# A gated recurrence on TensorE: the scores within 32 tokens in one run of 32-column tiles per head

## The chip, the core and the metric

One core of a Trainium2 chip. The metric is the device time of one execution in microseconds (us), the median of three runs. The engines are PE (TensorE, its weight loads as PEld), DVE (VectorE), ACT (ScalarE), POOL (GpSimd) and SP (SyncE).

## What is computed

Two transformer-like blocks on 512 tokens of width 1024, in float32. The change lies in the first block's recurrence, which the reference evaluates chunk by chunk for eight heads with 128 channels each:

```
f = sigmoid(zf); k = 1 - f; q = silu(zq); g = log f
S_t = diag(f_t) S_{t-1} + k_t v_t^T          (per head, S is 128 x 128)
o_t = S_t^T q_t
y   = rmsnorm(o) * norm_g * silu(zo)
```

Written out, a token t takes from each earlier token s the score `sum_c q[t,c] k[s,c] exp(G[t,c] - G[s,c])`, with G the running sum of g, times v_s.

## The kernel before

Activations lie transposed: 128 channels on the partitions, 512 tokens along a row. A main product (`mm_T`, L202 to L204, and `mm_N`, L242 to L244) multiplies a weight block by the activations in three passes, each operand being a high and a low half in fp32r. A weight block is loaded by SP, its high half cast by ACT (`wh`, L181) and its low half subtracted by DVE (`wl`, L182).

**The recurrence.** The decay from s to t is split by halving levels. At level n the tokens are cut into blocks of 2 x 2^n; the keys of a block's first half are decayed up to its middle, the queries of its second half from there. `Core.decays(n)` makes this tile, `dec`: POOL subtracts (two instructions, levels 0 to 5), or DVE adds up sums (levels 6 to 8), ACT takes the exponential, and DVE, or POOL for levels 1 and 3, multiplies by keys and queries. A product of keys with queries gives the level's scores. `Core.diag()` makes the scores of a token with itself, `Core.level(n)` those of level n: for n < 5 four products, one for each 128 tokens, each of 128 key columns with 64 query columns into PSUM, after which DVE copies under a mask into the score tile `sd` (L724). Level 5 goes through column tiles of 32 (`p[u:u + 32]`, u being 0 or 64), level 6 through 64 columns; levels 7 and 8 have tiles of their own (`l1`, `l2`). `Core.values()` multiplies the scores by the values, then `square`, `norm` and `done` norm and gate the head's output.

**The order.** `weave` writes two streams side by side: `main()` has the input products of heads 1 to 7 (`head_in`: forget gate zf, query zq, output gate zo) and the first three gates of the branches; `side()` has the recurrence of the heads. Each side step yields a cost that paces it against the main stream (`HGW`). `look(n)` writes decays ahead of their use. A scheduler then orders each engine's instructions, mainly as they are written; on the chip every engine works through its own list in that order.

Of the kernel before, what the change touches and what calls it, by code (L numbers as in the profile page):

```python
# [8 lines left out]
F32 = mybir.dt.float32  # L9
# [16 lines left out]
# buffers: raw weights, split weights, 2 KB tiles, small tiles, pairs of tiles, tiles of the attention  # L26
N_RAW = 4
N_W = 6
N_T = 54
# [11 lines left out]
CS = (0, 2, 6)  # L41
# [16 lines left out]
def tile_two_blocks(ctx: ExitStack, tc: tile.TileContext, a: dict, out: bass.AP):  # L58
# [197 lines left out]
    def weave(main, side, mt, st, late=False):  # L256
        """Emits two streams side by side, each at the pace of its length on the tensor engine."""
# [32 lines left out]
    # plan of all weights in the order of use  # L290
# [70 lines left out]
    # the small vectors, a chunk of 128 to a row; the first norm's come first  # L361
# [161 lines left out]
    # masks of the decay levels  # L523
    LV = [1, 2, 4, 8, 16]
    masks = cp.tile([128, len(LV), 64], U8, name="masks")

    def make_masks():
        for n, h in enumerate(LV):
# [8 lines left out]
            pool.tensor_copy(masks[:, n, :], m)  # L537

# [119 lines left out]
    class Core:  # L658
        """One head of the recurrence: the decays of the halving levels, scores, values."""
# [6 lines left out]
        def decays(self, n):  # L666
# [4 lines left out]
            e = T("dec")  # L671
# [20 lines left out]
        def diag(self):  # L692
            kq = self.kq
            p = PS("lv")
            for b in range(NT):
                bs = slice(b * 128, (b + 1) * 128)
                pe.matmul(p[:, bs], lhsT=kq[:, 0, bs], rhs=kq[:, 1, bs], start=True, stop=True)
            self.sd = T("sd")
            tt(dve, pieces(self.sd, 128), pieces(p, 128), ident.unsqueeze(1).to_broadcast([128, NT, 128]))

        def level(self, n):
            t = self.dec.pop(n)
            p = PS("lv")
            if n == 6:
                for b in range(NT):
                    pe.matmul(p[:64, b * 64:(b + 1) * 64], lhsT=t[:, b * 128:b * 128 + 64],
                              rhs=t[:, b * 128 + 64:(b + 1) * 128], start=True, stop=True)
                act.copy(pieces(self.sd, 128)[:64, :, 64:128], pieces(p[:64, :256], 64))
            elif n == 5:
                for b in range(2 * NT):  # L710
                    u = 64 * (b % 2)
                    pe.matmul(p[u:u + 32, b // 2 * 32:b // 2 * 32 + 32], lhsT=t[:, b * 64:b * 64 + 32],
                              rhs=t[:, b * 64 + 32:b * 64 + 64], start=True, stop=True)
                for u in (0, 64):
                    act.copy(pieces(self.sd, 128)[u:u + 32, :, u + 32:u + 64], pieces(p[u:u + 32, :128], 32))
            elif n < 5:
                hh = 1 << n
                nb = 64 // hh
                tv, sv = (z.rearrange("p (b q j i) -> p b q j i", b=NT, j=2, i=hh)[:, :, :, 1, :] for z in (t, self.sd))
                for b in range(NT):  # L720
                    pe.matmul(p[:, b * 64:(b + 1) * 64], lhsT=t[:, b * 128:(b + 1) * 128], rhs=tv[:, b],
                              start=True, stop=True)
                mk = masks[:, n, :].rearrange("p (q i) -> p q i", i=hh).unsqueeze(1).to_broadcast([128, NT, nb, hh])
                dve.copy_predicated(sv, mk, p[:, :256].rearrange("p (b q i) -> p b q i", b=NT, i=hh))  # L724
            elif n == 7:
                for b in range(2):
                    pe.matmul(p[:, b * 128:(b + 1) * 128], lhsT=t[:, b * 256:b * 256 + 128],
                              rhs=t[:, b * 256 + 128:b * 256 + 256], start=True, stop=True)
                self.l1 = T("l1", (128, 256))
                act.copy(self.l1, p[:, :256])  # L730
            else:
                for b in range(2):
                    pe.matmul(p[:, b * 256:(b + 1) * 256], lhsT=t[:, b * 128:(b + 1) * 128], rhs=t[:, 256:512],
                              start=True, stop=True)
                self.l2 = T("l2")
                act.copy(self.l2, p)
# [47 lines left out]
    def side():  # L784
# [13 lines left out]
        for h in range(8):  # L798
# [5 lines left out]
            look(9 * h + AHEAD)  # L804
# [3 lines left out]
            c.diag()  # L808
            yield 870
            for n in range(9):  # L810
                if ahead[0] <= 9 * h + n:
                    look(9 * h + n + 1)
                c.level(n)
                look(9 * h + n + 1 + AHEAD)
                yield 435 if 5 <= n < 8 else 870
                if h and n == CS[0]:
                    cores[h - 1].square()
                if h and n == CS[1]:
                    cores[h - 1].norm()
                if h and n == CS[2]:  # L820
                    cores.pop(h - 1).done()
# [36 lines left out]
    open_x(8)  # L858
    run(zi_half(0))
# [191 lines left out]
    # block-diagonal ones, causal mask, selector of a head's row  # L1051
# [15 lines left out]
    # f: log of the forget gates, summed over the tokens  # L1067
# [303 lines left out]
```

## Time and profile before

| | |
|---|---|
| median of three runs | 2157.38 us (2157.03 to 2157.44) |
| span of the profiled execution, first to last instruction | 2155.2 us |
| that execution's own time beside it | not recorded apart from the span |
| PE busy / DVE busy | 2119.9 us (98%) / 1243.4 us (58%) |
| ACT busy / POOL busy | 879.5 us (41%) / 522.9 us (24%) |
| first score product of head 0 / last of head 7 | 124.5 us / 359.0 us |

Busy shares are of the span. The shares of the whole span mix the recurrence, which has much work for DVE and POOL, with long stretches of plain products that have little.

### The profile page before, as it was taken

Reading aid. Unit: us, or ns where it says so; the run is one execution under the profiler, and the core shown is the slowest. Engines: PE = TensorE matmul, PEld = TensorE weight load, DVE = VectorE, ACT = ScalarE, POOL = GpSimd, SP = SyncE. Lnnn points to the kernel's source line nnn. Section 1 sums busy time; section 2 is a strip of 40 time slices with the busy share of each in tenths; the row PEclk is TensorE's granted clock in tenths of the full one; section 3 lists DMA queues with packets and bytes.
Section 4 is the critical chain, followed back from the end, with each engine's and each line's share of the span. In section 5 each row is a group of like instructions: output and inputs, shape, how many; then the busy total and the mean of one; then the engine's idle time right before and its main releaser. Section 6 shows DMA issues by size and latency. Waiting matters only on the chain.

```text
span 2155.2 us, 24922 instructions
## 1 busy us (share of the span) xinstructions
PE 2119.9 (98%) x9984; PEld 1739.5 (81%) x9984; DVE 1243.4 (58%) x1605; ACT 879.5 (41%) x1349; POOL 522.9 (24%) x446
## 2 busy tenths in 40 slices
PE   9999999999999999899999999999999999999999
PEld 7888777888888888688888888878877778888887
DVE  5588896555344443654555454568587755545453
ACT  6455555544323323332333232345466653323232
POOL 2537664012222222530111010020024411101000
PEclk9999999999999999999999999999999999999999
DMA  6311111232233332132322232232211112323321
GB/s 217 98 62 57 40 59 59 98 108 89 97 98 98 98 98 85 52 118 78 118 79 98 98 101 95 83 114 79 95 43 40 59 59 79 98 98 98 98 88 49
DMA packets 179180, 187.38 MB, mean 87 GB/s; under 512 B 4379, under 2 KB 169976, under 8 KB 179064
## 3 DMA queue, kind: packets, MB, share of 16 engines
q1 hardware_dynamic: 179048, 185.79, 26.6%
q8 instruction: 78, 1.28, 0.2%
q14 instruction: 38, 0.31, 0.0%
q10 hardware_dynamic: 16, 0.00, 0.0%
HBM read 183.68 MB, written 2.10 MB: 86 GB/s over the span
## 4 chain that ended last, share of the span: by engine, by line
PE 85%; DVE 7%; POOL 3%; ACT 3%; issue 2%; DMA 0%; SPq 0%; DVEq 0%; POOLq 0%; ACTq 0%
PE mm L202 25%; PE mm L203 25%; PE mm L204 25%; PE ao L1282 2%; POOL dec L107 2%; PE mn L244 1%; PE mn L243 1%; PE mn L242 1%; DVE wl L182 1%; ACT e L120 1%; DVE dec L107 1%; DVE sc L107 1%; PE pt L1270 1%; DVE e L110 1%; PE sc L1244 1%
## 5 line engine op out<-in xcount | busy, mean ns | idle before, releaser
L202 PE MATMUL mm<-xh,wh 128*128 128x512 f32 x2552 | 1006.6, 395 | 5.9 <-ACT xh L120 5.2
L203 PE MATMUL mm<-xl,wh 128*128 128x512 f32 x2552 | 999.2, 392 | 0.7 <-DVE xl L110 0.6
L204 PE MATMUL mm<-xh,wl 128*128 128x512 f32 x2552 | 998.5, 392 | 0.5 <-DVE wl L182 0.5
L181 ACT CAST wh<-raw 128x1024 fp32r<-128x1024 f32 (+2 forms) x355 | 363.5, 1025 | 783.5 <-PE mm L203 688.4
L182 DVE TENSOR_TENSOR wl<-raw,wh 128x1024 fp32r<-128x1024 f32 (+2 forms) x355 | 466.3, 1315 | 179.1 <-ACT wh L181 175.2
L202 PEld LDWEIGHTS mm<-xh,wh 128*128 128x128 f32 x2552 | 481.2, 189 | 106.9 <-ACT xh L120 6.1
L204 PEld LDWEIGHTS mm<-xh,wl 128*128 128x128 f32 x2552 | 480.6, 188 | 102.6 <-DVE wl L182 1.0
L203 PEld LDWEIGHTS mm<-xl,wh 128*128 128x128 f32 x2552 | 480.9, 188 | 100.5 <-DVE xl L110 2.0
L107 POOL TENSOR_TENSOR ua<-ua,rb 128x512 f32<-128x512 f32 x44 | 57.3, 1302 | 592.6 <-ACT ua L120 592.6
L107 DVE TENSOR_TENSOR x<-mm,x 128x512 f32<-128x512 f32 x64 | 44.1, 690 | 153.3 <-PE mm L204 153.3
L107 POOL TENSOR_TENSOR dec<-sc 128x256 f32<-128x256 f32 x96 | 89.5, 958 | 41.5 <-ACT kq L120 20.9
L107 DVE TENSOR_TENSOR a<-mm,rb 128x512 f32<-128x512 f32 x44 | 30.4, 691 | 103.5 <-PE mm L204 103.5
L107 POOL TENSOR_TENSOR acc<-acc,sq 128x512 f32<-128x512 f32 x42 | 62.8, 1495 | 103.9 <-ACT sq L120 82.0
L107 POOL TENSOR_TENSOR rl<-rl 128x512 f32<-128x512 f32 x32 | 49.0, 1532 | 129.3 <-ACT rl L120 129.3
L107 DVE TENSOR_TENSOR sg<-mm,ua 128x512 f32<-128x512 f32 x44 | 30.4, 690 | 84.3 <-POOL ua L107 81.8
L114 POOL TENSOR_SCALAR pe<-pe,rs 128x128 f32<-128x128 f32 (+1 forms) x32 | 31.1, 971 | 188.9 <-DVE rs L1262 184.1
L107 POOL TENSOR_TENSOR x<-x,rs 128x512 f32<-128x512 f32 x32 | 48.6, 1518 | 113.8 <-DVE rs L107 113.8
L110 DVE SCALAR_TENSOR_TENSOR xl<-x,vecs,xh 128x512 fp32r<-128x512 f32 x48 | 63.5, 1327 | 15.3 <-ACT xh L120 15.2
L110 DVE SCALAR_TENSOR_TENSOR ua<-a,convs,ua 128x511 f32<-128x511 f32 x88 | 65.8, 747 | 4.8 <-ACT ua L120 3.3
L242 PE MATMUL mn<-wh,xh 128*128 128x512 f32 x160 | 63.5, 404 | 0.0
L120 ACT ACTIVATE ua<-ua 128x512 f32<-128x512 f32 x44 | 27.8, 632 | 86.5 <-DVE ua L110 86.4
L243 PE MATMUL mn<-wl,xh 128*128 128x512 f32 x160 | 62.5, 391 | 0.0
(249 smaller groups left out, 2070.6 us busy)
## 6 DMA issues: line engine op xcount, KB each, us to landing
raw<-in_ffn_w_up_dram SPq DMA_DIRECT2D x44, 1024.0 KB
raw<-in_w_ff_dram SPq DMA_DIRECT2D x32, 1024.0 KB
raw<-in_w_in_dram SPq DMA_DIRECT2D x26, 1024.0 KB
raw<-in_ffn_w_down_dram SPq DMA_DIRECT2D x18, 1024.0 KB
raw<-in_a_w_in_dram SPq DMA_DIRECT2D x12, 1024.0 KB
raw<-in_w_kvf_dram SPq DMA_DIRECT2D x8, 1024.0 KB
raw<-in_b_w_qg_dram SPq DMA_DIRECT2D x8, 1024.0 KB
raw<-in_w_up_b_dram SPq DMA_DIRECT2D x4, 1024.0 KB
```

The lines of the kernel that those rows point to most:

```text
L107: e.tensor_tensor(out=o, in0=i0, in1=i1, op=op)
L110: dve.scalar_tensor_tensor(out=o, in0=i0, scalar=s, in1=i1, op0=op0, op1=op1)
L114: e.tensor_scalar(out=o, in0=i, scalar1=s1, scalar2=None, op0=op0)
L120: act.activation(out=o, in_=i, func=func, scale=scale, bias=bias, **kw)
L181: act.copy(hi, src)
L182: ins = dve.tensor_tensor(out=lo, in0=src, in1=hi.bitcast(F32), op=ALU.subtract)
L202: pe.matmul(ps, lhsT=lh, rhs=rh, start=start, stop=False)
L203: pe.matmul(ps, lhsT=lh, rhs=rl, start=False, stop=False)
L204: pe.matmul(ps, lhsT=ll, rhs=rh, start=False, stop=stop_)
L242: pe.matmul(pss[j], lhsT=xh[:, t0], rhs=wh[:, kk, :], start=(k + kk == 0), stop=False)
L243: pe.matmul(pss[j], lhsT=xh[:, t0], rhs=wl[:, kk, :], start=False, stop=False)
L1282: pe.matmul(o[64 * hA:64 * hA + 64, tb * 128:(tb + 1) * 128], lhsT=v[j][h // 8][:, (h % 8) * 64:(h % 8) * 64 + 64], rhs=et[:, j * 128:(j + ...
```

## The change

Diagonal and levels 0 to 4 (all scores within 32 tokens) become one run, `small()`: for each 32 tokens one product of 32 key columns, put into one of four column tiles of the array (32 partitions of PSUM each), with 32 query columns for the diagonal and 16 for a level. All scores of the run lie in one PSUM tile, 128 + 5 x 64 columns wide. DVE gathers them into a tile `s32` of 128 x 128 (one product with a folded identity, five copies under masks), and four copies, two on DVE and two on ACT, put them into `sd`. Levels 5 and 6 become a second run, `mid()`, level 6 now in two column tiles of 32; levels 7 and 8 a third, `far()`, unchanged but for the order. All five decays of the first run are written ahead of it. The decays get eight buffers of their own and the score tiles two, which are zeroed once; the pool of shared tiles goes from 54 to 51. The yielded costs and the pace follow the new steps.

```
-N_T = 54
+N_T = 51
-HGW = (130, 76)
+N_DEC = 8
+HGW = (130, 60)
...
-            e = T("dec")
+            e = xp[-1].tile([128, 512], F32, tag="dec", bufs=N_DEC, name=nm("dec"))
...
-        def diag(self): ...
-        def level(self, n): ...
+        def small(self):
+            kq = self.kq
+            p = PS("lv")
+            for b in range(NT):
+                for g in range(4):
+                    q = slice(b * 128 + 32 * g, b * 128 + 32 * g + 32)
+                    pe.matmul(p[32 * g:32 * g + 32, b * 32:b * 32 + 32], lhsT=kq[:, 0, q], rhs=kq[:, 1, q],
+                              start=True, stop=True)
+            for n in range(5):
+                t = self.dec.pop(n)
+                for b in range(NT):
+                    for g in range(4):
+                        q = slice(b * 128 + 32 * g, b * 128 + 32 * g + 32)
+                        c0 = 128 + 64 * n + 16 * b
+                        pe.matmul(p[32 * g:32 * g + 32, c0:c0 + 16], lhsT=t[:, q],
+                                  rhs=halves(t[:, q], 1 << n)[:, :, 1, :], start=True, stop=True)
+            s32 = T("s32", (128, 128))
+            tt(dve, pieces(s32, 32), pieces(p[:, :128], 32), id32.unsqueeze(1).to_broadcast([128, NT, 32]))
+            for n in range(5):
...
+                dve.copy_predicated(sv, mk, p[:, c0:c0 + 64].rearrange("p (b q i) -> p b q i", b=NT, i=hh))
+            self.sd = sds[self.h % len(sds)]
+            for g in range(4):
+                u = slice(32 * g, 32 * g + 32)
+                (act.copy if g % 2 else dve.tensor_copy)(pieces(self.sd, 128)[u, :, u], pieces(s32, 32)[u])
+        def mid(self):
+            p = PS("lv")
+            t5, t6 = self.dec.pop(5), self.dec.pop(6)
...
+            for b in range(NT):
+                for g in range(2):
+                    pe.matmul(p[32 * g:32 * g + 32, 128 + b * 64:192 + b * 64],
+                              lhsT=t6[:, b * 128 + 32 * g:b * 128 + 32 * g + 32],
+                              rhs=t6[:, b * 128 + 64:(b + 1) * 128], start=True, stop=True)
...
         for h in range(8):
-            look(9 * h + AHEAD)
+            look(9 * h + 5)
...
+            c.small()
+            yield 3200
...
+            look(9 * h + 7)
+            c.mid()
+            yield 700
...
+            look(9 * h + 9)
+            c.far()
+            yield 1300
...
+            look(9 * h + 9 + AHEAD)
             c.values()
```

On PE, head 0, between main products (`mm`), before: level 0 (`dec_953`) and level 1 (`dec_958`); `lv` is a score tile in PSUM.

```order
L721 MATMUL lv_1175<-dec_953 128x64 x4
L202 MATMUL mm_1146<-xh_353,wh_1059 128x512
L203 MATMUL mm_1146<-xl_354,wh_1059 128x512
L204 MATMUL mm_1146<-xh_353,wl_1060 128x512
L202 MATMUL mm_1204<-xh_145,wh_1102 128x512
L203 MATMUL mm_1204<-xl_146,wh_1102 128x512
L204 MATMUL mm_1204<-xh_145,wl_1103 128x512
L721 MATMUL lv_1208<-dec_958 128x64 x4
```

The same place in the changed kernel: diagonal (L704) and levels 0 to 4 (L712) in one piece.

```order
L204 MATMUL mm_1167<-xh_225,wl_1081 128x512
L704 MATMUL lv_1180<-kq_814 32x32 x16
L712 MATMUL lv_1180<-dec_969 32x16 x16
L712 MATMUL lv_1180<-dec_974 32x16 x16
L712 MATMUL lv_1180<-dec_979 32x16 x16
L712 MATMUL lv_1180<-dec_984 32x16 x16
L712 MATMUL lv_1180<-dec_989 32x16 x16
L202 MATMUL mm_1167<-xh_257,wh_1080 128x512
```

What were six runs with main products between them is one run of 96 products. Level 4, whose decay used to be needed last, now stands in the same run as the diagonal.

On POOL, the decays of head 5, before; the instructions that read `sc` are the two differences of a level, those that read `kq` the products of levels 1 and 3.

```order
L107 TENSOR_TENSOR dec_2365<-sc_2092 128x256 x2
L107 TENSOR_TENSOR dec_2370<-sc_2092 128x128x2 x2
L107 TENSOR_TENSOR dec_2375<-sc_2092 128x64x4 x2
L107 TENSOR_TENSOR dec_2388<-sc_2092 128x32x8 x2
L107 TENSOR_TENSOR dec_2370<-dec_2370,kq_2091 128x512
L107 TENSOR_TENSOR dec_2464<-sc_2092 128x16x16 x2
L107 TENSOR_TENSOR dec_2388<-dec_2388,kq_2091 128x512
```

The same in the changed kernel; the sixth row is level 5's, `osl` belongs to the norm of the head before.

```order
L107 TENSOR_TENSOR dec_2786<-sc_2418 128x256 x2
L107 TENSOR_TENSOR dec_2791<-sc_2418 128x128x2 x2
L107 TENSOR_TENSOR dec_2796<-sc_2418 128x64x4 x2
L107 TENSOR_TENSOR dec_2801<-sc_2418 128x32x8 x2
L107 TENSOR_TENSOR dec_2806<-sc_2418 128x16x16 x2
L107 TENSOR_TENSOR dec_2987<-sc_2418 128x8x32 x2
L107 TENSOR_TENSOR dec_2791<-dec_2791,kq_2417 128x512
L107 TENSOR_TENSOR osl_2650<-osq_2647,osh_2649 128x512
L107 TENSOR_TENSOR dec_2801<-dec_2801,kq_2417 128x512
```

The product of level 1 moved behind the differences of levels 4 and 5, that of level 3 behind these and `osl`.

## Rows read from the trace of the kernel before

**Rows 1.** The page, busy us, share of the span and instructions of each engine.
```profile
PE 2119.9 (98%) x9984; PEld 1739.5 (81%) x9984; DVE 1243.4 (58%) x1605; ACT 879.5 (41%) x1349; POOL 522.9 (24%) x446
```

**Rows 2.** Windows: length, busy us of PE, PEld, DVE, ACT, POOL; clock, DMA share, GB/s.
```profile
124.00:235.00 111.00, 110.64 (x682) 93.90 (x682) 94.97 (x122) 60.34 (x104) 61.62 (x58) 1.00 0.24 77
235.00:330.00 95.00, 85.49 (x513) 71.23 (x512) 89.04 (x108) 52.60 (x94) 60.21 (x54) 0.98 0.13 43
330.00:365.00 35.00, 32.65 (x189) 26.79 (x188) 28.04 (x38) 18.59 (x36) 17.99 (x17) 0.95 0.15 47
```

**Rows 3.** Waits, 235 to 330 us: who waited for whom, us in all, times, longest.
```profile
PE lv L733 <- DVE dec L107: 4.4, 2, 2.5
```

**Rows 4.** Timeline of PE: start us, us, line, operation; xN is so many instructions.
```profile
193.35 0.39 PE L243 MATMUL mn<-wl,xh 128*128 128x512 f32 x1
193.58 1.00 PE L721 MATMUL lv<-dec 128*128 128x64 f32 x8
...
194.70 0.39 PE L242 MATMUL mn<-wh,xh 128*128 128x512 f32 x1
...
195.85 0.40 PE L244 MATMUL mn<-wh,xl 128*128 128x512 f32 x1
196.18 0.45 PE L712 MATMUL lv<-dec 128*32 128x32 f32 x16
...
196.90 0.40 PE L243 MATMUL mn<-wl,xh 128*128 128x512 f32 x1
197.13 0.39 PE L244 MATMUL mn<-wh,xl 128*128 128x512 f32 x1
197.45 0.68 PE L706 MATMUL lv<-dec 128*64 128x64 f32 x8
...
198.40 0.39 PE L243 MATMUL mn<-wl,xh 128*128 128x512 f32 x1
```

**Rows 5.** Groups of PE by form, 90 to 365 us: busy us, mean ns of one.
```profile
L721 PE MATMUL lv<-dec 128*128 128x64 f32 x320 | 40.4, 269 | 2.6 <-DVE dec L107 2.4
L706 PE MATMUL lv<-dec 128*64 128x64 f32 x64 | 5.4, 227 | 0.2 <-DVE dec L107 0.2
L712 PE MATMUL lv<-dec 128*32 128x32 f32 x128 | 3.6, 199 | 0.0
```

**Rows 6.** Groups of DVE by form, 235 to 330 us.
```profile
L724 DVE COPY_PREDICATED sd<-masks,lv 128x256 f32<-128x256 uint8 x15 | 8.2, 550 | 0.1
L107 DVE TENSOR_TENSOR sd<-lv,ident 128x512 f32<-128x512 f32 x3 | 2.0, 677 | 0.0
```

**Rows 7.** Groups of DVE by form, whole span.
```profile
L1248 DVE TENSOR_REDUCE nmx<-sc 128x1 f32<-128x512 f32 x16 | 10.9, 681 | 5.6 <-PE sc L1246 5.6
L1248 DVE TENSOR_REDUCE nmx<-sc 128x1 f32<-128x128 f32 x16 | 4.6, 287 | 13.2 <-PE sc L1246 13.2
```

**Rows 8.** Timeline of POOL, 262 to 279 us.
```profile
262.45 7.35 POOL L107 TENSOR_TENSOR dec<-sc 128x256 f32<-128x256 f32 x8
...
272.15 2.26 POOL L107 TENSOR_TENSOR dec<-sc 128x256 f32<-128x256 f32 x2
...
275.05 1.67 POOL L107 TENSOR_TENSOR dec<-dec,kq 128x512 f32<-128x512 f32 x1 [0.63 <-ACT dec L120]
```

**Rows 9.** Timeline of DVE, 267 to 280 us.
```profile
269.21 0.68 DVE L107 TENSOR_TENSOR zf<-mm,rb 128x512 f32<-128x512 f32 x1
...
276.09 1.71 DVE L648 TENSOR_TENSOR_SCAN sc<-reset,g 128x512 f32<-128x512 f32 x1
```

**Rows 10.** The page, DMA queue of PE's instructions: packets, MB, share.
```profile
q8 instruction: 78, 1.28, 0.2%
```

**Rows 11.** Timeline of PE, 285 to 287 us.
```profile
285.45 0.40 PE L204 MATMUL mm<-xh,wl 128*128 128x512 f32 x1
285.81 0.45 PE L712 MATMUL lv<-dec 128*32 128x32 f32 x16
```

More of the change, by code (lines that the diff above doesn't have):

```diff
@@ L38 @@
 AHEAD = 4
+N_DEC = 8
 HGSTART = 36
-HGW = (130, 76)
-CS = (0, 2, 6)
+HGW = (130, 60)
 MUL_POOL = (1, 3)
@@ L524, in tile_two_blocks @@
     LV = [1, 2, 4, 8, 16]
-    masks = cp.tile([128, len(LV), 64], U8, name="masks")
+    masks = cp.tile([128, len(LV), 16], U8, name="masks")
+    id32 = cp.tile([128, 32], F32, name="id32")
     def make_masks():
+        dve.tensor_reduce(out=id32, in_=ident.rearrange("p (g c) -> p c g", g=4), axis=AX.X, op=ALU.max)
         for n, h in enumerate(LV):
@@ L536, in make_masks @@
                                pattern=[[2 * h, nb], [0, h]], channel_multiplier=-1)
-            pool.tensor_copy(masks[:, n, :], m)
+            r = SM("mr", 16)
+            dve.tensor_reduce(out=r, in_=m.rearrange("p (g c) -> p c g", g=4), axis=AX.X, op=ALU.max)
+            pool.tensor_copy(masks[:, n, :], r)
     gbc, bbc, sbc, wsn = T("lng"), T("lnb"), T("bs"), T("wsn")
@@ L690, in decays @@
             self.dec[n] = e
-        def diag(self):
+        def small(self):
             kq = self.kq
@@ L695, in diag @@
             for b in range(NT):
[L696 to L702, printed above, removed]
-            p = PS("lv")
[L704 to L736, printed above, removed]
@@ new lines, in small @@
+            self.sd = sds[self.h % len(sds)]
[3 more added lines that the diff above has]
+        def mid(self):
+            p = PS("lv")
+            t5, t6 = self.dec.pop(5), self.dec.pop(6)
+            for b in range(2 * NT):
+                u = 64 * (b % 2)
+                pe.matmul(p[u:u + 32, b // 2 * 32:b // 2 * 32 + 32], lhsT=t5[:, b * 64:b * 64 + 32],
+                          rhs=t5[:, b * 64 + 32:b * 64 + 64], start=True, stop=True)
+            for b in range(NT):
[3 more added lines that the diff above has]
+                              rhs=t6[:, b * 128 + 64:(b + 1) * 128], start=True, stop=True)
+            for u in (0, 64):
+                act.copy(pieces(self.sd, 128)[u:u + 32, :, u + 32:u + 64], pieces(p[u:u + 32, :128], 32))
+            act.copy(pieces(self.sd, 128)[:64, :, 64:128], pieces(p[:64, 128:384], 64))
@@ new lines, in far @@
+        def far(self):
+            t = self.dec.pop(7)
+            p = PS("lv")
+            for b in range(2):
+                pe.matmul(p[:, b * 128:(b + 1) * 128], lhsT=t[:, b * 256:b * 256 + 128],
+                          rhs=t[:, b * 256 + 128:b * 256 + 256], start=True, stop=True)
+            self.l1 = T("l1", (128, 256))
+            act.copy(self.l1, p[:, :256])
+            t = self.dec.pop(8)
+            p = PS("lv")
+            for b in range(2):
+                pe.matmul(p[:, b * 256:(b + 1) * 256], lhsT=t[:, b * 128:(b + 1) * 128], rhs=t[:, 256:512],
+                          start=True, stop=True)
+            self.l2 = T("l2")
+            act.copy(self.l2, p)
@@ L807, in side @@
                     yield None
[L808 to L821, printed above, removed]
+            c.small()
+            yield 3200
+            if h:
+                cores[h - 1].square()
+            look(9 * h + 7)
+            c.mid()
+            yield 700
+            if h:
+                cores[h - 1].norm()
+            look(9 * h + 9)
+            c.far()
+            yield 1300
+            if h:
+                cores.pop(h - 1).done()
+            look(9 * h + 9 + AHEAD)
             c.values()
@@ L858, in tile_two_blocks @@
     open_x(8)
+    sds = [xp[-1].tile([128, 512], F32, tag="sd", bufs=2, name=nm("sd")) for _ in range(2)]
+    for t in sds:
+        pool.memset(t, 0.0)
     run(zi_half(0))
```

5 lines of the change are left out of this document (added).

## Prediction

> **What bounds the kernel now.** I read the page's busy line first, then the windows around the recurrence, then single runs of products in the order of time.
>
> The busy line has TensorE at 98% of the span [rows 1]. A busy PE isn't a PE at its peak, so that row alone would let one think that any instruction taken off TensorE shortens the kernel. The windows show where that holds. I cut the recurrence near the first scores of heads 0, 4 and 7 [rows 2]. In the first window (four heads, 111 us) PE is busy for 110.64 us and DVE for 94.97, that is 86%: TensorE sets the pace. In the second (three heads, 95 us) PE falls to 85.49 and DVE rises to 89.04, 94%: there TensorE waits for VectorE, which has the decays' products, the weights' low halves and the gates to do. One wait shows it: the last level's products stand for VectorE's decay for 4.4 us in that window [rows 3]. In the third (35 us, head 7) neither is full. After it the program is plain products, which the change doesn't touch.
>
> So a microsecond saved on TensorE counts whole in the first window and hardly in the second, where one saved on VectorE counts instead.
>
> **What a run of scores costs now.** In the order of time, the main products start 0.23 us apart (196.90 to 197.13), and a level of a head is a run put between them [rows 4]. Its cost is the time from the main product ahead of it to the second one behind it, less two steps of 0.23. For one of the levels 0 to 4: 193.35 to 194.70 is 1.35, less 0.46 is 0.89, say 0.90. For level 5: 195.85 to 196.90 is 1.05, so 0.59. For level 6: 197.13 to 198.40 is 1.27, so 0.81. The diagonal has as many loads of 128 columns as a level, and I take 0.90 for it too. Per head: 6 x 0.90 + 0.59 + 0.81 = 6.8 us.
>
> **The new run, TensorE.** A product in f32 stands as two instructions (320 for the 160 calls of the levels 0 to 4 [rows 5]). The new first run has 16 products for the diagonal and 16 for each of five levels: 96 products, 192 instructions, each with 32 columns to load. The trace has one row of that form, level 5. Its 16 instructions lie in 0.45 us with a mean of 0.199 for one [rows 4, 5], so they start over 0.25 us, 15 gaps of 16.7 ns. The same sum for level 6 (64 columns) gives 0.68 - 0.227 = 0.45 over 7 gaps, 65 ns, and for a small level (128 columns) 1.00 - 0.269 = 0.73 over 7, 104 ns. From 64 to 32 columns the gap falls to a quarter, although the columns only halve. Level 5 alternates between two column groups (u = 0 or 64), level 6 doesn't: I read the other half as two column tiles working abreast. The new run turns through four groups, so its gap is between 16.7 ns (two abreast, as seen) and half of that, 8.3 (four abreast, argued, not seen); upwards the nearest row is level 6's 65. I take 16.7, the only row of this form: 192 x 16.7 ns = 3.2 us. The edges of such a run (what level 5 costs beyond its gaps) are 0.59 - 0.25 = 0.34. Together 3.5 us.
>
> The second run holds level 5 (0.25) and level 6 as 16 instructions that load 32 columns and stream 64, on two groups: 65 / 2 = 33 ns each, 0.52; one pair of edges, 0.34. Together 1.1 us. Levels 7 and 8 and the values are unchanged. In heads 4 to 7 the order puts one or two pieces of other work inside the first run, up to two more pairs of edges, 0.7 us, mostly in the window that VectorE sets; I leave them out. TensorE's bill falls from 6.8 to 4.6 us a head: 2.2 us, 17.6 for eight heads. Four abreast it is 1.9 + 1.1, so 3.8 us a head.
>
> **VectorE and ScalarE.** Now a head takes one product with the identity (0.68) and five predicated copies of 256 elements at 0.55, so 3.4 us [rows 6]. Afterwards these are one operation on 128 elements, five on 64, and two copies of 32 x 128; ScalarE takes two more copies, which it has room for. For the size I use the maxima, the same shape in 128 and 512 elements: 0.287 and 0.681 us [rows 7], so 1.03 ns an element and 0.155 fixed. That prices the first at 0.29, a copy at 0.29 at most, and a predicated copy between 0.155 + 0.066 = 0.22 and 0.55 - 192 x 1.03 ns = 0.35. The sum lies between 2.0 and 2.6; I take 2.3, a saving of 1.1 us a head.
>
> **What is moved.** Levels 0 to 4 used to be a run each, spread between main products, and a run needed only its own decay. Now the one run needs all five decays. What stands behind it on TensorE is every main product, so a late decay stops everything. GpSimd is the engine to look at: it makes the differences (eight in 7.35 us, two more in 2.26) and multiplies levels 1 and 3 (1.67 for one) [rows 8]. In the order of the changed kernel level 5's two differences stand ahead of these two products, so from the end of the scan to the last decay of the run are 7.35 + 2.26 + 2.26 + 2 x 1.67 = 15.2 us. Ahead of that lie VectorE's steps from the forget gate's product to the end of the scan, among other work: 269.21 to 277.80, 8.6 us [rows 9]. Together that's some 23.8 us, against about 26 us from one head's run to the next (a quarter of the first window as the sum below leaves it, 103.7 us). The forget gate's product of the next head ends just behind the run of this one. So the decays come just in time, and I charge 1.5 us of new waits to the first window, where nothing else would hide them. Moving the decays and score tiles into buffers of their own, and 51 instead of 54 shared tiles, I cost at nothing: the order behind the recurrence is the same but for single rows. If the tiles ran short, GpSimd's decays would start later and add to those 1.5 us.
>
> **Sum.** First window: 4 heads x 2.2 = 8.8, less 1.5, so 7.3 us; VectorE would then be at 90.6 of 103.7, 87%, still no bound. Second: VectorE's 89.04 less 3 x 1.1 is 85.7, at its present 94% a window of 91.5 instead of 95: 3.5 us. Third: head 7's own 2.2. Together 13.0 us. The profiled span of 2155.2 becomes 2142.2. The median of the runs lies 2.2 above that span, which I leave as it is: 2157.4 - 13 = 2144.4, so 2144 us.
>
> **Rivals.**
> *Four abreast.* For it speaks level 5's row: with two groups in turn the gap is a quarter of that with 64 columns. Against it: no row has four. First window 4 x 3.8 = 15.2 less 2 of waits (VectorE would be at 93%), second 4, third 3.8: 21 us, so 2136.
>
> *The waits eat the gain.* If GpSimd's 15.2 us come later than I put them, every head's run waits. At 1.6 us a head, 12.8 for eight, the 13 us are gone: 2157, the same. For it speaks the slack of some two microseconds; against it, that in the second window TensorE idles anyhow.
>
> *The long run is fed too slowly: slower.* The run is 384 instructions with the loads; the longest burst of this form that the trace shows has 32, and a burst can lie ready in a queue. TensorE's instructions come in packets, 78 of them with 1.28 MB in the span [rows 10], 16 KB each; for the 19,968 products and loads of the busy line that's 64 bytes each, 256 in a packet. One run is one and a half packets. It decides at 6.8 - 1.1 - 0.34 = 5.4 us for the 192, 28 ns an instruction. At 40 ns the run is 8.0 us, a loss of 2.3 a head and 18 us: 2176; at level 6's 65 ns a loss of 7.1 a head: 2214. Against it speaks a run of level 5 that came on an empty engine: at 285.81, 0.36 us behind the last start where 0.23 would do, its 16 still lie in 0.45 us [rows 11]. That run wasn't fed from a stock, but it was short.
> The Trainium skill, page "TensorE: Matmul & The Clock Gate", section "Back-to-back issue gap", gives small products a floor of about 25 ns from start to start whatever their size, and about 62 ns where the sequencer decodes them in software. By the first the run would be an estimated 5.1 us and the kernel some 5 us faster at most, by the second 12.2 us and the kernel about 50 us slower. This case's trace doesn't agree with either for a burst of 16 (16.7 ns); for 192 in a row no run here shows it.
>
> **How the numbers follow.** Chances: the sum as forecast, 7 to 19 us faster, 0.50; four abreast 0.18; waits that eat the gain 0.20, half of it within the bound; slow feeding 0.12. About 0.2% (4.3 us) is what a measurement of this kernel can tell from no change. Faster: 0.50 + 0.18 + 0.10 = 0.78; same 0.10; slower 0.12. The forecast's own range is 2138 to 2150. To leave out no more than two in ten it must take in most of four abreast and of the waits: 2131 to 2156.
>
> **What would show it.** Right: the first run's instructions start some 17 ns apart, and the run stands between main products for about 3.5 us; the predicated copies take 0.25 to 0.35; the time from the first scores of head 0 to those of head 4 falls by about 7 us, from there to head 7 by 3 to 4. Wrong: gaps above 28 ns, or holes inside the run; TensorE idle ahead of it, released by GpSimd's decays; no shorter second window, which would say that something other than VectorE's work sets it.

## The result and the profile after

The changed kernel takes 2181.91 us (median of 4 runs, 2179.91 to 2182.8) against 2157.2 of the kernel before: a ratio of 1.0114, interval 1.01 to 1.0129. It is slower by some 25 us where 13 us less were forecast. The profiled execution has a span of 2181.1 us, 25.9 above that of before.

Windows of the changed kernel, cut at the first scores of heads 0, 4 and 7 as in [rows 2] (length, busy us of PE, PEld, DVE, ACT, POOL, clock, DMA share, GB/s):
```profile
125.00:242.60 117.60, 103.48 (x1282) 84.11 (x1281) 95.89 (x134) 65.60 (x117) 66.33 (x65) 0.91 0.23 73
242.60:359.80 117.20, 84.40 (x989) 67.47 (x988) 84.71 (x116) 58.53 (x107) 61.80 (x57) 0.88 0.12 37
```
Cut exactly at the first scores, the windows before were 110.7 and 95.0, so 6.9 and 22.2 us are lost here. From head 7's scores to the first product of the norm that closes the mixer (the closing norm) it is 211.8 instead of 215.4, a gain of 3.6; behind that, 1609.5 against 1609.7. TensorE is less busy than before in both windows: it has less to do and waits more. The waits of PE from 124 to 385 us (in all, times, longest) say for what:
```profile
PE oss L789 <- ACT osh L784: 32.7, 5, 10.2
PE o L778 <- ACT l L753: 8.0, 5, 2.9
PE lv L712 <- issue: 4.2, 2, 2.3
```
`oss` is the norm product of the head before, `osh` the rounded square of its output. Neither was priced in the forecast. One such wait in the order of time, first PE, then ACT:
```profile
260.37 0.39 PE L204 MATMUL mm<-xh,wl 128*128 128x512 f32 x1
269.32 0.80 PE L789 MATMUL oss<-osh,onesr 128*128 128x512 f32 x1 [8.56 <-ACT osh L784]
269.92 1.06 PE L750 MATMUL lv<-dec 128*128 128x128 f32 x4
270.77 1.91 PE L757 MATMUL lv<-dec 128*128 128x256 f32 x4
```
```profile
262.82 0.63 ACT L120 ACTIVATE kq<-e 128x512 f32<-128x512 f32 x1 [1.21 <-DVE e L110]
263.64 0.63 ACT L120 ACTIVATE e<-zc 128x512 f32<-128x512 f32 x1 [0.18 <-DVE zc L114]
...
266.62 0.63 ACT L120 ACTIVATE dec<-dec 128x512 f32<-128x512 f32 x1 [1.31 <-POOL dec L107]
267.15 0.61 ACT L120 ACTIVATE sg<-e 128x512 f32<-128x512 f32 x1
267.67 0.58 ACT L120 ACTIVATE osq<-o 128x512 f32<-128x512 f32 x1
...
268.67 0.60 ACT L784 CAST osh<-osq 128x512 fp32r<-128x512 f32 x1
```
Look at `osq`, the square of the head before. Its input `o` was ready at 246.7 us, when the last values product ended. But on ScalarE it stands behind steps of the next head: the gate chain (`kq`, `e`, `sg`), which waits for VectorE (1.21 and 0.18 us), and two exponentials of decays, one of which waits 1.31 us for GpSimd. So it starts at 267.67. The change writes the square behind the whole first run and its 3200 columns, where the kernel before wrote it 1740 columns into the head; by then the weave has placed products of the next head, and so their gates, ahead of it. The norm product follows 700 columns later, ahead of the far levels, and behind it on TensorE stands everything. A wait can cost more than its length. Of these two stretches behind it, the first begins with the norm product:
```profile
269.30:274.00 4.70, 4.67 (x16) 4.06 (x17) 3.50 (x4) 2.41 (x4) 4.70 (x6) 0.62 0.00 0
274.00:278.00 4.00, 4.00 (x19) 3.30 (x18) 4.00 (x3) 0.00 (x0) 3.72 (x3) 1.00 0.00 0
```
After nearly nine idle microseconds the granted clock has a mean of 0.62 for 4.7 us (part of it at the lower of the two levels, 1.2 GHz) and is back at 1.00 (2.4 GHz) behind that.

The run itself is cheap. Timeline of PE around an undisturbed first run, and VectorE's merges by form, to set beside [rows 4 to 6]:
```profile
213.59 0.39 PE L204 MATMUL mm<-xh,wl 128*128 128x512 f32 x1
213.91 0.46 PE L704 MATMUL lv<-kq 128*32 128x32 f32 x32
214.19 1.62 PE L712 MATMUL lv<-dec 128*32 128x16 f32 x160
215.74 0.50 PE L202 MATMUL mm<-xh,wh 128*128 128x512 f32 x1
216.07 0.40 PE L203 MATMUL mm<-xl,wh 128*128 128x512 f32 x1
```
```profile
L712 PE MATMUL lv<-dec 128*32 128x16 f32 x1280 | 15.5, 189 | 4.2 <-issue 4.2
...
L722 DVE COPY_PREDICATED s<-masks,lv 128x64 f32<-128x64 uint8 x40 | 10.2, 254 | 0.9
```
By the forecast's own measure the run costs 216.07 - 213.59 - 0.46 = 2.02 us. The 160 instructions of the levels (80 products) lie in 1.62 us, 0.189 for one: (1.62 - 0.189) / 159 = 9.0 ns from start to start.

Not every run goes through like that. Heads 0 and 2 have a hole inside, in which TensorE waits for nothing that the profile shows. This is head 0's:
```profile
125.05 0.46 PE L704 MATMUL lv<-kq 128*32 128x32 f32 x32
125.32 1.45 PE L712 MATMUL lv<-dec 128*32 128x16 f32 x140
129.09 0.37 PE L712 MATMUL lv<-dec 128*32 128x16 f32 x20 [2.32 <-issue]
```
With their holes of 2.3 and 1.8 us these two runs take 4.4 and 3.9 us from first to last, those of heads 1 and 3 take 1.9. A packet of the queue that brings PE's instructions starts at 126.37 and at 187.92 us, 0.4 and 0.5 us ahead of the two holes; in heads 1 and 3 none starts before the run's last 0.3 us. In heads 4 to 6 the run is broken up by the values of the head before, which wait for their copies `l` inside it (0.7, 2.3 and 1.4 us).

### The profile page after: what moved, and what is told of

Its sections match the earlier page's. It is cut to its first block, busy times and chain, and to the rows that moved or that the text cites. A ratio compares the mean times of both kernels' runs of the same rounds, so it can differ in the third digit from the quotient of the medians.

```text
span 2181.1 us, 27350 instructions
## 1 busy us (share of the span) xinstructions
PE 2106.0 (97%) x11200; PEld 1720.9 (79%) x11200; DVE 1234.4 (57%) x1627; ACT 880.8 (40%) x1362; POOL 515.5 (24%) x448
## 4 chain that ended last, share of the span: by engine, by line
PE 87%; DVE 6%; POOL 3%; ACT 2%; issue 1%; DMA 0%; SPq 0%; POOLq 0%; DVEq 0%; ACTq 0%
PE mm L202 25%; PE mm L203 25%; PE mm L204 25%; PE ao L1310 2%; PE mn L243 2%; PE mn L244 2%; PE mn L242 2%; POOL dec L107 2%; DVE dec L107 1%; PE pt L1298 1%; DVE wl L182 1%; DVE sc L107 1%; POOL x L107 1%; PE sc L1272 1%; PE ml L229 1%
## 5 line engine op out<-in xcount | busy, mean ns | idle before, releaser
L107 POOL TENSOR_TENSOR dec<-sc 128x256 f32<-128x256 f32 x96 | 82.5, 892 | 75.0 <-DVE sc L652 51.8
L107 DVE TENSOR_TENSOR dec<-dec,kq 128x512 f32<-128x512 f32 x56 | 55.5, 1012 | 17.0 <-ACT dec L120 16.2
```

Of the source, the lines that this page charges most:

```text
L107: e.tensor_tensor(out=o, in0=i0, in1=i1, op=op)
```

## The experiments

For each kernel: time; the stretches from head 0 to 4, from 4 to 7, from 7 to the closing norm, by the first scores in its profiled execution; their sum. The kernel before was run beside each group of experiments and took 2157.0 to 2158.5 us, so a difference of one or two microseconds between two rows says nothing. The stretches from 4 to 7 and from 7 on have the same main products in most rows but trade time with each other: together they are 310 us in before, e1_runs_apart and e3_apart_buf.

```
                          us      0-4    4-7   7-norm    sum
before                  2157.2   110.7   95.0   215.4   421.0
after                   2181.9   117.6  117.2   211.8   446.5
e1_sq_early             2161.4   112.3  100.8   212.7   425.7
e1_norm_late            2178.3   110.0  114.5   215.1   439.6
e1_old_tiles            2186.9   121.0  116.1   212.6   449.7
e3_before_cs            2187.8   119.8  114.0   217.0   450.8
e1_runs_apart           2157.9   111.0  100.7   208.9   420.6
e2_apart_twice          2174.1   119.3  101.6   217.5   438.4
e3_apart_buf            2157.5   111.0   95.5   214.6   421.1
e3_apart_ahead5         2152.1   106.3   97.9   210.3   414.6
e4_before_ahead5        2159.6   111.3   97.9   214.7   423.9
e4_no_merge             2158.0   104.9  100.2   211.4   416.5
e5_mul_dve              2144.8   103.3   93.6   211.5   408.4
e5_pairs                2152.8   104.9   97.0   214.4   416.3
```

**What makes the loss.** Theory A: the new places of square and norm. Rivals: the long run is dear in itself (B); five decays are wanted at once (C). Four kernels are to tell them apart. The square ahead of the first run, nothing else:
```
+            if h:
+                cores[h - 1].square()
             c.small()
             yield 3200
-            if h:
-                cores[h - 1].square()
```


> One edit to the changed kernel: the square of the head before (ScalarE, with the copy that follows it) is issued ahead of the first run of a head instead of behind its 3200 columns; its norm product stays ahead of the run of the two far levels. Theory A (order: TensorE stands at the norm product because ScalarE reaches the square only behind the next head's gate chain; 32.7 us of waits in five places of the changed kernel): these waits all but vanish, the first scores of heads 0 to 7 lie about 200 to 205 us apart instead of 235, and the time is 2145 to 2160. Theory B (the long run of 192 small products is itself too dear): nothing changes, 2178 to 2186. Theory C (five decays wanted at once: TensorE and GpSimd wait on each other at the first run): the norm waits go but the same time comes back ahead of the run, 2170 or more.

2161.39 us, ratio 1.0019 (1.0009 to 1.0028). 20 of the 25 us are back, a little less than A said (the scores of heads 0 and 7 lie 213 us apart, not 200 to 205); C, which had the time come back ahead of the run, falls. The waits of PE from 125 to 385 us:
```profile
PE mm L202 <- ACT xh L478: 7.9, 1, 7.9
PE lv L712 <- issue: 6.3, 3, 2.5
PE mn L242 <- DVE z L107: 5.1, 1, 5.1
PE o L778 <- ACT l L753: 4.7, 4, 1.9
PE oss L789 <- ACT osh L784: 3.3, 1, 3.3
```
The norm wait fell from 32.7 to 3.3; other waits took its place, the longest 7.9. The holes given as issue are now three, 6.3 us in all, more than the 3 to 4 us by which this kernel is still behind the kernel before; each begins 0.4 to 0.6 us behind the start of a packet of PE's instructions. What the kernel would take without them was not tried.

The norm product behind the far levels, the square still late:
```
-            if h:
-                cores[h - 1].norm()
             look(9 * h + 9)
             c.far()
             yield 1300
             if h:
-                cores.pop(h - 1).done()
+                cores[h - 1].norm()
             look(9 * h + 9 + AHEAD)
             c.values()
+            if h:
+                cores.pop(h - 1).done()
```


> One edit to the changed kernel: the norm product of the head before is issued behind the run of the two far levels instead of ahead of it, and what follows it behind the values; the square stays late on ScalarE. Theory A: TensorE has the far run and some 1300 columns of main products more before it stands, so part of the 32.7 us of waits goes, at most about 5 x 1.8 us; but the chain on ScalarE is as late as before: 2165 to 2180. If the place of the product alone were to blame and not the square's place on ScalarE: 2150 to 2160. Theory B and C: 2178 to 2186.

2178.26 us, ratio 1.0095. That time lies within A's range and just within that of B and C, so it doesn't choose between them; it rules out that the place of the product alone is to blame. The wait, of which A wanted a part gone, stays whole, with 2000 columns between square and norm product:
```profile
PE oss L789 <- ACT osh L784: 34.6, 5, 14.1
```

The order of the change with the 128-column products and merges of before (`mid` then calls levels 5 and 6, `far` 7 and 8):
```
         def small(self):
+            self.diag()
+            for n in range(5):
+                self.level(n)
```


> The order of the changed kernel (one run for the diagonal and levels 1 to 16, one for 32 and 64, square behind the first, norm ahead of the far levels) with the products of the kernel before, 128 columns wide, and its masks. Theory A: as slow as the changed kernel or slower, 2180 to 2210, with the wait at the norm product of 25 us or more in sum. Theory B: the loss goes with the small tiles, so 2150 to 2165.

2186.88 us, ratio 1.014, with the norm wait in it:
```profile
PE oss L780 <- ACT osh L775: 26.6, 5, 9.5
```
The loss is there without one small tile, and B falls. The small tiles save 5 us in this order.

And the other way round, the kernel before with nothing but this, which writes the square of the head before behind level 3 instead of 0, its norm product behind level 4 instead of 2:
```
-CS = (0, 2, 6)
+CS = (3, 4, 6)
```


> The kernel before with three numbers changed and nothing else: the square of the head before is issued behind level 3 of the next head instead of level 0 (45% of the head's columns instead of 18%), its norm product behind level 4 instead of level 2; the last step stays. No product, mask or decay changes. Theory A (the place of square and norm alone makes the loss): 2172 to 2190, with 20 us or more of waits of TensorE at the norm product. If the loss needs the single long run too: 2155 to 2165.

2187.83 us, ratio 1.0144 (1.0127 to 1.0161). Two numbers, no product touched, and 31 us are lost: A holds without the long run, although the new places are not quite those of the change. The waits are not as expected: PE stood 11.9 us at the norm product, not 20, and 6.5 at the values, where it hadn't stood before; its waits for decays fell from 11.1 to 6.2. Its windows from head 0 to 4 and 4 to 7:
```profile
124.50:244.30 119.80, 114.17 (x687) 96.36 (x686) 88.13 (x119) 60.55 (x104) 55.52 (x54) 0.99 0.22 71
244.30:358.20 113.90, 98.47 (x536) 80.82 (x535) 88.90 (x114) 56.49 (x99) 65.24 (x59) 0.91 0.12 38
```
In the second, PE is 13 us busier than in [rows 2], at a clock of 0.91 instead of 0.98. It has 24 main products more there, 5.5 us at 0.23 each; the scores and values are the same, so some 7 us are left. Part of a wait's price appears as busy time.

**Where the tiles' gain is.** With the loss explained, the question is why the cheap run gave nothing. The small tiles in the old order, the diagonal and each level a run of its own, level 6 as before, square and norm in their old places:
```
+            c.diag()
+            yield 870
+            for n in range(9):
...
+                c.level(n)
```


> The small tiles of the changed kernel (four 32-column tiles abreast for the scores within 32 tokens) in the order of the kernel before: the diagonal and each level a run of its own, square and norm where they stood before, four decays ahead, level of 64 as before. Theory A (order, not tiles): no norm wait over 2 us, TensorE about 0.3 us cheaper for each of six runs of a head and VectorE's merges on 64 elements instead of 256: 2130 to 2150. Theory B (small products too dear in themselves): six short runs of 32 products each cost as much as the one of 192, so 2175 or more.

2157.89 us, ratio 0.9999 (0.999 to 1.0009), outside both expectations. A run of 16 small products (32 instructions) costs 0.58 where 128-column products cost 0.90, and not a microsecond is seen. The waits from 124 to 385 us:
```profile
PE o L768 <- ACT l L744: 9.4, 3, 5.9
PE o L768 <- ACT l L750: 4.7, 1, 4.7
PE o L768 <- DVE sd L726: 3.4, 1, 3.4
```
By this list, TensorE's saving is given back at the values, 17.5 us of waits for late copies; e3_apart_buf below shows that this can't be all. More room ahead of the values, the same order:
```
-                yield 435 if 5 <= n < 8 else 870
+                yield 435 if 5 <= n < 8 else 2000 if n == 8 else 870
...
             c.values()
-            yield 2180
+            yield 1050
```


> The small tiles in the order of before (e1_runs_apart, 2157.9 us, where TensorE waited 17.5 us at the values for ScalarE's copies l and VectorE's sd) with 2000 instead of 870 columns of main products ahead of the values and 1050 instead of 2180 behind them. Theory A2 (TensorE's saving of about 15 us is given back at these waits): the waits fall under 5 us and the time is 2140 to 2150. Rival (the stretch is bounded by VectorE and by the in-order chain between VectorE and ScalarE, TensorE's saving is off the path): the waits move elsewhere, 2154 to 2161.

2158.0 us, as the rival said, but not because the waits moved: those at the values fell only to 13.5, and the one at the input of a main product rose from 2.6 to 7.1. So the edit didn't take away what it was meant to. Two like edits in the changed order with the square early gave nothing either: more columns ahead of the values (2161.17, with the waits there up from 7.4 to 16.6), and the next head's decays one by one (2161.47):
```
-            yield 1300
+            yield 2400                 e2_early_slack; behind the values 1080
-            look(9 * h + 9 + AHEAD)
+            look(9 * h + 10)           e2_early_spread; + 11, 12 and 13 further on
```


> The changed kernel with the square early (as in e1_sq_early, 2161.4 us) and one more edit: between the run of the far levels and the values stand 2400 columns of main products instead of 1300, and 1080 instead of 2180 behind the values. Theory A2 (what is left after the square is moved is waits of TensorE for ScalarE's late copies l and sd ahead of the values product, 7.4 us, plus the 7.9 us at an input of the next main product which is late for the same reason): the value waits go, 2150 to 2157. Theory D (VectorE's bursts are what is left: TensorE's pieces wait where VectorE must read a finished product first): no change, 2158 to 2165.

> The changed kernel with the square early (2161.4 us) and one more edit: the four decays of the next head that were issued all together behind the far levels are issued one by one over the same columns of main products. Theory D (bursts: five decays behind each other on VectorE, 6 to 7 us in the chain of waits, hold up the reading of main products): 2148 to 2157. Theory A2: no change, 2158 to 2165.

Each small product issued twice (`for _ in range(2):` around both):

> The small tiles in the order of before (2157.9 us) with each of the 192 small products of a head issued twice; the output stays the same. It prices TensorE's columns: alone the second 192 take 8 x 6 x about 0.37 = 18 us. If TensorE bounds the stretch: 2170 to 2177. If its time there is off the path: 2157 to 2163. A run price as for instructions one after the other (rival: products fed too slowly, 28 ns or more each) would be 43 us, so 2185 or more.

2174.14 us: 16 us for the second 192 instructions of each head. By the table, 8.2 us of it lie between heads 0 and 4 and 9.5 behind head 4. So TensorE's time is on the path in this kernel, in both stretches: made dearer it costs at once. Made cheaper it gave nothing; that something else of nearly the same length takes over is the likely reading, not a shown one.

The decays back in the common pool, 55 buffers instead of 8 of their own:
```
-            e = xp[-1].tile([128, 512], F32, tag="dec", bufs=N_DEC, name=nm("dec"))
+            e = T("dec")
```


> The small tiles in the order of before (2157.9 us) with the decays in the common pool of small tiles again (55 buffers) instead of 8 buffers of their own. In the run with 8 of its own GpSimd stood 37 us at decays for TensorE's reading of an old one, with squares and gates queued behind. Theory E (those 8 buffers eat the gain): the GpSimd wait falls under 10 us and the time is 2142 to 2152. Otherwise (VectorE and ScalarE's in-order chain bounds): 2154 to 2161.

2157.46 us: buffers were not it. The waits did change, though. GpSimd's 37.0 us of waits for TensorE to read an old decay are gone, and of TensorE's 17.5 us at the values this is left:
```profile
PE o L768 <- ACT l L744: 0.4, 1, 0.4
```
Instead TensorE waits for VectorE's decays (13 us) and at the norm product (5.3), and the time is the same. So the waits at the values say where the saving went in one order, not why it was lost. GpSimd's half of the square one level later, and six decays ahead instead of four, gave nothing either (2161.52 and 2156.93, both outside what was expected):
```
+                if h and n == CS[0] + 1:
+                    cores[h - 1].rest()        e3_apart_osl: osl stands here
-AHEAD = 4
+AHEAD = 6                              e4_ahead6
```


> As e3_apart_buf, and GpSimd's half of the split square (osl) is issued one level later, so that GpSimd has a decay to do while ScalarE makes its input (before: 23 us of GpSimd waits there, 52 us with the small tiles). If GpSimd's queue holds up the decays: 3 to 8 us below e3_apart_buf. If not: within 3 us of it.

> Small tiles, order of before, six decays ahead. In the run with five TensorE still stood 13.7 us for decays of VectorE and GpSimd. If lead is what is lacking: 2145 to 2150. If VectorE has no more to give: 2150 to 2156.

The first of these two needs 418.7 us up to the closing norm, 2.4 less than e3_apart_buf, and loses 5.5 behind it, where the code is the same; e4_no_merge, below, loses as much there. Why, stays open.

Five decays ahead instead of four, with the small tiles and with the old ones:
```
-AHEAD = 4
+AHEAD = 5
```


> As e3_apart_buf with five decays ahead instead of four. If TensorE's runs now come too early for the elementwise engines, more lead gives the waits at the values back: 3 to 8 us below e3_apart_buf. If VectorE's share bounds the stretch, the same or up to 5 us above, since decays then stand ahead of the gate chain that main products wait for.

> Control: the kernel before with five decays ahead instead of four, old products and masks. If the 5 us that five ahead gave with the small tiles (2152.1) is lead alone: also 2150 to 2154 here. If it is the tiles' saving becoming usable: 2155 to 2162 here.

2152.14 us with the tiles (ratio 0.9972, 0.9961 to 0.9983), 2159.64 with the old ones (1.0012). So it isn't lead as such: at five ahead the tiles are worth 7.5 us, at four nothing. Five is one setting, however; at six the gain is gone again (2156.93), so how much of it is a lucky order of instructions was not told apart. The windows of the first, head 0 to 4 and 4 to 7:
```profile
124.90:231.30 106.40, 105.14 (x1260) 79.94 (x1259) 86.25 (x127) 62.10 (x111) 60.43 (x55) 0.98 0.24 78
231.30:329.20 97.90, 83.24 (x944) 63.00 (x943) 89.48 (x117) 57.46 (x106) 65.80 (x57) 0.91 0.14 47
```
Most of the gain is in the first, 110.7 to 106.3, where TensorE is full; the second is longer than before, with DVE busy for 89.48 us although its merges are cheaper.

Is VectorE's work the bound there? The merges of levels 1, 2, 4 and 8 left out:
```
-                dve.copy_predicated(sv, mk, p[:, :64]...
+                (dve.copy_predicated if n == 4 else lambda *_: None)(sv, mk, p[:, :64]...
```


> Small tiles, order of before, five ahead (2152.1), with the merges of levels 1, 2, 4 and 8 left out, so that part of the scores is missing: it prices VectorE's time, about 8 x 4 x 0.25 = 8 us less on VectorE, nothing less on TensorE. If VectorE's share bounds the stretch of heads 0 to 7: 2143 to 2148. If it is TensorE or a lead: 2150 to 2154.

2158.03 us, slower than both expectations; in the profiled executions 5.5 us of the difference lie behind the closing norm. Up to that norm it is 416.5 against 414.6. So 8.1 us of VectorE's instructions are gone and nothing is gained: 1.5 us less from head 0 to 4, 3.4 more behind that. The window from head 4 to 7:
```profile
229.50:329.70 100.20, 83.27 (x944) 62.50 (x943) 88.34 (x107) 57.92 (x107) 68.02 (x59) 0.91 0.15 51
```
12 of the 32 merges lay in it, 3.0 us, and DVE's busy time fell by 1.1. So less work for VectorE does not shorten this stretch. Nor is its busy time a count of its work: one instruction can take twice as long as another of the same form. VectorE's products of the decays have one form and very different durations (min/median/max), in the kernel before and in e3_apart_ahead5:
```profile
L107 DVE TENSOR_TENSOR dec<-dec,kq x54: 674/792/1907, 130.1 to 357.5; 128x512 f32<-128x512 f32 x54
L108 DVE TENSOR_TENSOR dec<-dec,kq x53: 674/1082/1800, 130.5 to 348.3; 128x512 f32<-128x512 f32 x53
```
In the order of time in e3_apart_ahead5, first DVE, then POOL:
```profile
245.72 1.61 DVE L108 TENSOR_TENSOR dec<-dec,kq 128x512 f32<-128x512 f32 x1
...
249.53 0.68 DVE L108 TENSOR_TENSOR dec<-dec,kq 128x512 f32<-128x512 f32 x1
...
251.24 0.69 DVE L108 TENSOR_TENSOR dec<-dec,kq 128x512 f32<-128x512 f32 x1
...
257.14 0.69 DVE L108 TENSOR_TENSOR dec<-dec,kq 128x512 f32<-128x512 f32 x1 [0.27 <-ACT dec L121]
...
266.35 1.25 DVE L108 TENSOR_TENSOR dec<-dec,kq 128x512 f32<-128x512 f32 x1
...
270.23 1.15 DVE L108 TENSOR_TENSOR dec<-dec,kq 128x512 f32<-128x512 f32 x1
```
```profile
244.55 2.24 POOL L108 TENSOR_TENSOR osl<-osq,osh 128x512 fp32r<-128x512 f32 x1
258.47 1.28 POOL L108 TENSOR_TENSOR gate<-gate,or 128x512 f32<-128x512 f32 x1 [11.69 <-PE lv L729]
...
263.13 9.34 POOL L108 TENSOR_TENSOR dec<-sc 128x256 f32<-128x256 f32 x10
```
From 246.79 to 258.47 GpSimd is idle, and the product takes 0.68; beside GpSimd it takes 1.15 to 1.61. Over 100 to 400 us of this trace, the 22 with GpSimd idle for over nine tenths of their time have a median of 0.68, the 26 with it busy for over eight tenths 1.17.

So GpSimd's share was moved both ways, level 5's product to GpSimd, and both of GpSimd's to VectorE:
```
-MUL_POOL = (1, 3)
+MUL_POOL = (1, 3, 5)      e4_mul_pool
+MUL_POOL = ()             e5_mul_dve
```


> As e3_apart_ahead5 with the product of level 32 moved from VectorE to GpSimd (idle for 70% of the run of these heads' waits): some 0.7 to 1.0 us a head less on VectorE. If VectorE bounds: 2145 to 2150. If GpSimd's longer chain delays the decays (each about 1.3 us there): 2153 to 2160.

> As e3_apart_ahead5 (2152.1), with GpSimd's products of two decays a head given to VectorE, so VectorE has 16 more of 0.68 us (11 us) and GpSimd 16 fewer of about 1.3 us. In the traces VectorE's decay products take 0.68 us while GpSimd is idle and 1.1 us (up to 1.9) while it runs. If that stretching is what holds VectorE back, GpSimd's smaller share pays for most of it: 2150 to 2155. If VectorE's own instructions bound the stretch of heads 4 to 7: 2156 to 2165.

More on GpSimd: 2154.58, in the range of the longer chain. None of these products on GpSimd: 2144.8 us, ratio 0.9937 (0.9924 to 0.9949), below both expectations and faster than both kernels. VectorE has 16 products more, and GpSimd only the differences of the decays. The windows from head 0 to 4 and 4 to 7:
```profile
125.20:228.50 103.30, 103.30 (x1260) 78.91 (x1262) 90.24 (x133) 62.16 (x111) 50.71 (x50) 1.00 0.25 81
228.50:322.00 93.50, 82.81 (x944) 63.42 (x943) 86.54 (x123) 57.77 (x106) 54.42 (x51) 0.91 0.15 48
```
TensorE doesn't wait in the first at all, and in the second DVE is busy for 3 us less than in e3_apart_ahead5 with more to do. Over the whole execution the sum of VectorE's durations rises by 3.9 us for 16 products more. The decays' products took 58.3 us and were 56, now they take 72.2 and are 72, so each is hardly cheaper (1.04 and 1.00 us). What fell, by 10 us, is other work, above all two steps ahead of the scan (`e<-zf` and `g<-zf,e`, 17.7 to 12.9). The edit does two things: it takes GpSimd from beside VectorE, and it shortens the chain of decays on GpSimd. Which gave more was not told apart, nor was it run with the old tiles, so what it gains on the kernel before (13.5 us by its own comparison, 2158.3) belongs to tiles, lead and this together.

The runs in pairs (diagonal with level 1, 2 with 4, 8 with 16), with five ahead:
```
             c.diag()
-            yield 870
+            yield 0
...
-                yield 435 if 5 <= n < 8 else 870
+                yield (1740, 0, 1740, 0, 1740, 435, 435, 435, 870)[n]
```


> As e3_apart_ahead5, with the runs taken in pairs: diagonal with level 1, levels 2 and 4, levels 8 and 16, without main products between them. A run of 64 small products measured 0.96 against two of 0.58, so 0.2 us a pair, 0.6 a head, 4.8 us in all on TensorE. If TensorE's stretch of heads 0 to 3 takes it: 2148 to 2151. If the decays come too late for pairs (they are wanted two at a time) or the rest is bounded elsewhere: 2152 to 2158.

2152.82 us, as the second expectation said: the first stretch falls to 104.9, the rest gives it back.

## Why the prediction was wrong, by its own steps

**The step that failed is "What is moved".** It followed GpSimd's decays to the first run, charged 1.5 us of waits there, and never priced the square and norm of the head before, which the change moves as well. The profile after shows no wait of a microsecond for decays and 32.7 us at the norm product. The rule that the engines work through their lists in order was applied to the decays alone. The runs put 31 us on such a move without the change (e3_before_cs), and 20 of the 25 come back when the square alone is moved (e1_sq_early). The rival of waits that eat the gain named the decays too, and its price ended at no change; none had waits for ScalarE, so nothing in the range reached 2182.

**The first run** was mis-sized on the safe side: 16.7 ns an instruction forecast, 9.0 measured, 2.02 us for 3.5 where the run is undisturbed. Four column tiles start about twice as often as two, as the rival said (8.3, 1.9 us). The second run was forecast at 1.1 us; by the same measure it took 1.02.

**Slow feeding** did not come as a price per instruction: 9.0 ns against the 28 at which it would decide. By the Trainium skill's floor of about 25 ns (page "TensorE: Matmul & The Clock Gate", section "Back-to-back issue gap") the 192 instructions would have taken an estimated 4.8 us; the trace does not agree, now for 160 in a row. But the sign that the forecast named, holes inside the run, is there in two of eight runs, 4.2 us in all, each just behind a packet of PE's instructions. That fits the rival's mechanism at a fraction of its price; the trace shows only which came first, and no run was made without the holes. They don't make the loss: e1_old_tiles loses as much without such holes. They may be what is left of it in e1_sq_early. The instructions' queue went from 78 packets [rows 10] to 88.

**VectorE's merges** were right: 0.254 us within 0.22 to 0.35. What they are worth was not: without most of them the kernel was no faster (e4_no_merge).

**The first window's term**, 7.3 us, agrees with the 7.4 of e5_mul_dve (4.3 in e3_apart_ahead5, 5.8 in e5_pairs), but by luck: it was 2.2 us a head less 1.5 for a joined run, and this is 24 short runs, each 0.32 cheaper (7.7). By its measured price the joined run would have been worth some 15 us there. That the gain needed five decays ahead, and GpSimd's products moved, was not foreseen.

**The second window's term** (VectorE's busy time falls, so the window falls) rested on a wrong reading of [rows 2]: a busy share of 94% was taken for the bound, as if busy time were work. With 3 us of merges left out of that window it got no shorter. 1.4 us were had in e5_mul_dve, not 3.5. And that a microsecond on TensorE hardly counts behind head 4 is not borne out: doubled, the small products cost as much there as ahead of it (e2_apart_twice).

**Buffers at nothing** held for the decays' eight (2157.9 with them, 2157.5 without), in the order of before.

## What to carry to other kernels

When a change joins runs, list every other step that the loop placed between them, and follow each on its own engine: a step that has its input long before still starts only when the list ahead of it is through, and what waits for it may hold the densest engine. Before a busy share is read as work, look at the spread of one form's durations; if it doubles beside another engine, moving work off that engine can be worth more than making work cheaper, as it was here (7.3 us, the shorter chain included). A list of waits shows where a saving went, not why: in e3_apart_buf the longest waits left and the time stayed. In a kernel whose engines are nearly balanced, try a saving at another lead before it is called worthless, and at a third before the gain is believed.

## What the hardware showed that was not expected

Instructions on four 32-column tiles in turn started every 9.0 ns, about half of the 16.7 of two groups. Ahead of each of the five holes inside such runs in after and e1_sq_early (1.8 to 2.5 us), a packet of PE's instructions had started 0.4 to 0.6 us earlier. VectorE's products of two SBUF tiles took 0.68 us alone and up to 1.80 beside GpSimd, while its product of `o`, which lies in PSUM, with a gate took 0.68 in both cases (6 and 2 of them in e3_apart_ahead5). The Trainium skill, page "SBUF — State Buffer", section "Who interferes with whom", says that an operation of VectorE with two SBUF inputs contends with a GpSimd instruction that reads SBUF, and one with at most one SBUF input, outside the modes that use two ports, does not; the trace agrees.
